# Up projection: pools laid out anew, sums of h behind h's own parts and two rows at once; down projection: low weight parts on VectorE

## The chip, the cores and the metric

The kernel runs on one core of one Trainium2 chip. The metric is the device time of one launch in microseconds. It was run three times, and the median counts.

## The reference, cut to what matters

A trunk of two layers for 1024 prompt frames and 8 x 16 sample frames (1152 columns in all, held as three chunks of 384), model width 1024, hidden width 4096. Layer 0 mixes with forgetting attention and causal pooling, layer 1 with stick-breaking attention. Behind each mixer stands the same MLP, which is what is changed:

```python
def _rmsnorm(x, g):
    xf = x.astype(jnp.float32)
    y = xf * lax.rsqrt(jnp.mean(xf * xf, axis=-1, keepdims=True) + EPS)
    return (y * g.astype(jnp.float32)).astype(x.dtype)

def _sq_relu_mlp(h, w_up, w_down):
    return jnp.square(jax.nn.relu(h @ w_up)) @ w_down
...
        h = _rmsnorm(x, norm_g[i, 1]) * (1 + sc2) + sh2
        x = x + g2 * _sq_relu_mlp(h, w_up[i], w_down[i])
```

## The kernel before

Every product is made in three passes: each fp32 operand is split into a high part (a cast on ACT) and a low part (the value less its high part, a subtraction on DVE or POOL), and PE adds high x high, high x low and low x high. The Tile framework's scheduler sets the order of each engine's queue from its own model of durations; `behind`, `at` and pins add constraints.

*Up projection* (`up_phase`, L516). The activations h lie in `xT`, feature rows on partitions, 8 rows k of 128. First the norm of each of the three chunks is made: squares on ACT (L367, L370), added up on DVE and POOL (L371) into `sa` and `sb`, joined (L372), summed over partitions by PE (L375), a square root on ACT (L381), a reciprocal on DVE (L382 to L385), and spread by PE (L392). `apply` (L533) multiplies by it on DVE (L535) and adds the shift on ACT (L536); the sample columns go through `samples` (L538) on DVE and POOL. The columns are then regrouped into four blocks of TB = 288: two halves tp, each with columns c = 1 and 2; feature rows are two halves r = 1 and 2 of four rows j.

`parts` (L546) makes a form's high part on ACT (L548) and its low part on DVE (L549), one row j at a time. The forms 11, 21, T4 and 22 are blocks of h themselves; T1, T2 and T3 come from `sums` (L567), seven-product (Strassen) sums of blocks, with subtractions on DVE (L565). The first four of 32 weight columns f are made by `plain` (L683), which needs only h's own blocks: a tile is 24 matmuls (L693), squared and clipped on ACT and DVE (L699, L700). The other 28 are taken two at a time, as 14 groups of seven products P1 to P7 (L629), each product with a weight form that DVE adds up from raw blocks (L565, L608). Raw blocks come over SP's queue (L583) into `u_raw` buffers (UR of them), and `w_parts` splits them: `u_hi` on ACT (L589), `u_lo` on POOL (L590), four buffers each. The results go to DRAM on ACT's queue (L637).

*Down projection* (`down_phase`, L765). The 32 rows f of the hidden layer are taken in rounds of (2, 2, 4, 4, 4, 4, 4, 4, 2, 2). For each f of a round SP loads the hidden row `hr` (128 x 3 x 384, three buffers) and the weight row `w_raw` (128 x 1024); `split` (L199) makes `w_hi` on ACT (L203) and `w_lo` on POOL (L204; on DVE for odd f below 4); `oh` is cast on ACT (L791), `ol` subtracted on DVE (L792), a chunk at a time; six buffers each. A pair of weight parts lies in one of three buffers of the weights' pool or three of `wx`. PE then makes 24 tiles a round (8 rows n by 3 chunks), each over all f of the round (L506), and `x_add` (L489) adds a tile to x on DVE (L492, for samples L496 and POOL's L498).

## Time and profile before

| | us |
|---|---|
| median of 3 runs (3207.66 to 3208.86) | 3208.78 |
| the profiled execution | 3204.72 |
| its span, which the trace covers | 3202.9 |
| PE busy in it | 3039.6 (95%) |
| DVE busy | 1778.7 (56%) |
| ACT busy | 1101.4 (34%) |
| POOL busy | 960.9 (30%) |

The mean granted clock of TensorE was 0.97 of full speed. Busy shares are means over stages with different limits: a stage is read from its windows (busy time of each engine and granted clock in a stretch) and from the list of waits (how long PE stood still, and what ended it). A busy PE at clock 0.50 does half the work of one at 1.00. The chain of work that ended last follows PE for the most part, so time that PE waits is time of the whole.

### The profile page before, as it was taken

What the parts mean: (1) busy time and instruction counts of PE and PEld (TensorE: products, weight loads), DVE (VectorE), ACT (ScalarE), POOL (GpSimd) and SP (SyncE); (2) the same over time, 40 slices, a digit from 0 to 9 for tenths busy, and PEclk for the clock granted to TensorE, in tenths of its full rate; (3) what the DMA queues carried; (4) which work ended last, traced back from release to release, by engine and by line L of the source; (5) the groups of instructions that cost most, each with busy time, mean ns of one, the idle gap of its engine ahead of it and who ended that gap; (6) DMA issues with size and microseconds to landing.
All of it is one profiled execution on the core that took longest, in us unless ns stands there. A gap on an engine that the chain in (4) does not pass through costs nothing. (4 is left out here: it accounts for less than half of the span.)

```text
span 3202.9 us, 54950 instructions
## 1 busy us (share of the span) xinstructions
PE 3039.6 (95%) x21422; PEld 2771.0 (87%) x21422; DVE 1778.7 (56%) x3500; ACT 1101.4 (34%) x2482; POOL 960.9 (30%) x801
## 2 busy tenths in 40 slices
PE   8999999979999999999999999999969999899898
...
GB/s 273 203 216 240 139 139 93 128 53 110 98 99 148 241 117 137 148 108 40 211 168 168 194 193 105 168 138 108 133 59 100 101 103 112 193 78 63 106 49 60
DMA packets 398792, 427.67 MB, mean 134 GB/s; under 512 B 41629, under 2 KB 349509, under 8 KB 398534
## 3 DMA queue, kind: packets, MB, share of 16 engines
...
## 5 line engine op out<-in xcount | busy, mean ns | idle before, releaser
L590 POOL TENSOR_TENSOR u_lo<-u_raw,u_hi 128x512 fp32r<-128x512 f32 x226 | 324.7, 1439 | 478.4 <-ACT u_hi L589 475.2
L204 POOL TENSOR_TENSOR w_lo<-w_raw,w_hi 128x1024 fp32r<-128x1024 f32 (+1 forms) x116 | 287.6, 2490 | 433.3 <-ACT w_hi L203 313.4
L498 POOL TENSOR_TENSOR xT<-xT,xs 128x128 f32<-128x128 f32 x224 | 117.7, 525 | 829.7 <-DVE xs L496 822.2
L203 ACT CAST w_hi<-w_raw 128x1024 fp32r<-128x1024 f32 (+1 forms) x120 | 125.7, 1051 | 645.9 <-PE ps_s L506 422.7
L492 DVE SCALAR_TENSOR_TENSOR xT<-ps_s,modT,xT 128x384 f32<-128x384 f32 (+1 forms) x372 | 210.6, 568 | 217.2 <-PE ps_s L506 215.9
L629 PE MATMUL ps_s<-FT,u_hi 128*128 128x288 f32 x1568 | 315.9, 295 | 0.0
L506 PE MATMUL ps_s<-ol,w_hi 128*128 128x384 f32 x792 | 267.7, 340 | 13.2 <-DVE ol L792 13.2
L506 PE MATMUL ps_s<-oh,w_hi 128*128 128x384 f32 x792 | 272.8, 344 | 0.7 <-DVE xT L492 0.4
L506 PE MATMUL ps_s<-oh,w_lo 128*128 128x384 f32 x792 | 270.7, 342 | 0.0
L589 ACT CAST u_hi<-u_raw 128x512 fp32r<-128x512 f32 x226 | 139.9, 621 | 354.5 <-PE ps_s L629 175.4
L629 PEld LDWEIGHTS ps_s<-FT,u_hi 128*128 128x128 f32 x1568 | 253.7, 189 | 0.0
L1173 DVE TENSOR_TENSOR_SCAN sn<-sn 128x128 f32<-128x128 f32 (+4 forms) x224 | 216.6, 995 | 45.2 <-ACT sn L1167 40.4
L629 PE MATMUL ps_s<-FT,u_lo 128*128 128x288 f32 x784 | 233.5, 298 | 4.8 <-POOL u_lo L590 4.8
L640 DVE TENSOR_TENSOR xT<-ps_s,xT 128x288 f32<-128x288 f32 x224 | 102.2, 457 | 219.1 <-PE ps_s L629 218.9
L1176 POOL TENSOR_TENSOR sg<-sg,sn 128x512 f32<-128x512 f32 (+3 forms) x112 | 136.2, 1216 | 260.6 <-DVE sn L1173 194.1
L792 DVE TENSOR_TENSOR ol<-hr,oh 128x384 fp32r<-128x384 f32 x192 | 192.0, 1053 | 19.7 <-ACT oh L791 19.6
L629 PE MATMUL ps_t<-F,u_hi 128*128 128x288 f32 x896 | 180.3, 294 | 2.6 <-ACT xT L656 2.6
L1241 ACT COPY pt<-ps_t 128x512 f32<-128x512 f32 (+3 forms) x256 | 126.2, 500 | 128.7 <-PE ps_t L1235 127.1
L492 DVE SCALAR_TENSOR_TENSOR xT<-ps_a,modT,xT 128x384 f32<-128x384 f32 (+1 forms) x180 | 102.2, 568 | 122.5 <-PE ps_a L506 121.8
L506 PE MATMUL ps_s<-w_hi,h 128*128 128x256 f32 (+1 forms) x800 | 159.2, 291 | 6.1 <-ACT h L466 3.4
L506 PEld LDWEIGHTS ps_s<-ol,w_hi 128*128 128x128 f32 x792 | 150.4, 190 | 15.7 <-DVE ol L792 15.7
L506 PEld LDWEIGHTS ps_s<-oh,w_hi 128*128 128x128 f32 x792 | 150.4, 190 | 14.8 <-issue 5.9
...
## 6 DMA issues: line engine op xcount, KB each, us to landing
...
```

Of the source, the lines that this page charges most:

```text
L203: after(nc.scalar.copy(hi[:, :n], raw[:, :n]), "act")
L204: after((eng or nc.gpsimd).tensor_tensor(lo[:, :n], raw[:, :n], hi[:, :n].bitcast(F32), op=ALU.subtract), "pool")
L492: nc.vector.scalar_tensor_tensor(xT[c][:, n, :npc], ps[:, :npc], g[:, n, 0:1], xT[c][:, n, :npc], op0=ALU.mult, op1=ALU.add)
L498: nc.gpsimd.tensor_tensor(xT[c][:, n, 256:], xT[c][:, n, 256:], t, op=ALU.add)
L506: mm = nc.tensor.matmul(ps, lhsT=a, rhs=b, start=(i == 0), stop=(i == n - 1))
L589: nc.scalar.copy(hi, src)
L590: nc.gpsimd.tensor_tensor(lo, src, hi.bitcast(F32), op=ALU.subtract)
L629: mm = nc.tensor.matmul(ps, lhsT=a[:, k, :], rhs=b[:, k, :], start=(start and i == 0), stop=(i == 11), skip_group_check=not start)
L792: nc.vector.tensor_tensor(ol[:, c], raw[:, c], oh[:, c].bitcast(F32), op=ALU.subtract)
L1173: nc.vector.tensor_tensor_scan(rev, rev, rev, initial=1.0, op0=ALU.mult, op1=ALU.bypass)
L1176: eng.tensor_tensor(sg[:, 0:m - 1], sg[:, 0:m - 1], sn[:, 1:m], op=ALU.mult)
L1241: nc.scalar.copy(pt.rearrange("p k n -> p (k n)")[:, 0:n], T[:, 0:n])
```

## The change

In the up projection: `apply` takes a whole chunk instead of pieces of 96 to 288 columns; `parts` and the sums take two rows j at once, so there are half as many, twice as wide; the first three subtractions of `sums` are put `behind` the latest low part of h's own blocks (`done["lo"]`); the norm's squares have two buffers; `u_raw` has five; and the pools are opened in another order and on other sides of the memory, with `u_out` in one of its own. In the down projection every `w_lo` of a hidden row is made on DVE, `wx` is used by f // 2, and `oh` and `ol` are made for all three chunks in one operation (in the first round in two). In the forget-attention one pool moves to the left side. The diff, without its blank lines:

```diff
@@ -62,7 +62,7 @@
 PIN_O = (5, 15)
 PIN_M = (4, 11)
 TB = 288
-UR = 6
+UR = 5
 UW = 4
 UG = 2
 UO = 3
@@ -521,18 +521,31 @@
         w = w_up[l]
         forms = ("11", "21", "T2", "T1", "T3", "22", "T4")
         with ExitStack() as es:
-            ur = es.enter_context(tc.tile_pool(name=f"ur{l}", bufs=1, side="right", reuse_waits="tile"))
-            uf = [es.enter_context(tc.tile_pool(name=f"uf{l}{tp}", bufs=1, reuse_waits="tile",
-                                                **({"side": "right"} if tp == 0 else {}))) for tp in range(2)]
-            uw = es.enter_context(tc.tile_pool(name=f"uw{l}", bufs=UW, side="right", reuse_waits="tile"))
-            F = {f: [[uf[tp].tile([P, 4, TB], F32R, name=f"F{f}{i}", tag=f"F{f}{i}") for i in range(2)] for tp in range(2)]
-                 for f in forms}
-            np_ = Npool(ur, {"sa": 1, "sb": 1, "nw": 1, "rc": 2})
-            def apply(c, sd, k, c0, c1):
-                x = xT[c][:, k, c0:c1]
-                nc.vector.scalar_tensor_tensor(x, x, A[:, k, 0:1], sd[:, c0:c1], op0=ALU.mult, op1=ALU.mult)
+            def pool(name, side="left", bufs=1):
+                return es.enter_context(tc.tile_pool(name=f"{name}{l}", bufs=bufs, side=side, reuse_waits="tile"))
+            def form_tiles(pools):
+                return {f: [pl.tile([P, 4, TB], F32R, name=f"F{f}{i}", tag=f"F{f}{i}") for i in range(2)] for f, pl in pools.items()}
+            ufa = pool("ufa")
+            F1 = form_tiles({f: ufa for f in forms[:4]})
+            uo = pool("uo")
+            uo.tile([P, TB], F32, name="u_out", tag="out", bufs=UO)
+            uw = pool("uw", bufs=UW)
+            ufb = pool("ufb")
+            F1.update(form_tiles({f: ufb for f in forms[4:]}))
+            ur = pool("ur", "right")
+            uf = pool("uf", "right")
+            F0 = form_tiles({f: uf for f in forms})
+            F = {f: (F0[f], F1[f]) for f in forms}
+            np_ = Npool(ur, {"sa": 1, "sb": 1, "nw": 2, "rc": 2})
+            def apply(c, sd, k):
+                x = xT[c][:, k, :CW if c < 2 else 256]
+                nc.vector.scalar_tensor_tensor(x, x, A[:, k, 0:1], sd[:, :CW if c < 2 else 256], op0=ALU.mult, op1=ALU.mult)
                 nc.scalar.activation(x, x, AF.Identity, bias=B[:, k, 0:1])
             def samples(sd, k0, k1):
@@ -544,37 +557,37 @@
                 nc.gpsimd.tensor_tensor(w4, w4, B[:, k0:k1, 1:9].unsqueeze(3).broadcast_to([P, n, NB, NT]), op=ALU.add)
             def parts(form, tp, j, src):
-                hi, lo = (t[:, j, :] for t in F[form][tp])
+                hi, lo = (t[:, j:j + 2, :] for t in F[form][tp])
                 nc.scalar.copy(hi, src)
-                nc.vector.tensor_tensor(lo, src, hi.bitcast(F32), op=ALU.subtract)
+                return nc.vector.tensor_tensor(lo, src, hi.bitcast(F32), op=ALU.subtract)
             def blk(tp, j, r, c):
                 t0 = (2 * tp + c - 1) * TB
-                return X[:, j + 4 * (r - 1), t0:t0 + TB]
-            def first_forms(tp, j):
-                parts("11", tp, j, blk(tp, j, 1, 1))
-                parts("21", tp, j, blk(tp, j, 2, 1))
-            def second_forms(tp, j):
-                parts("T4", tp, j, blk(tp, j, 1, 2))
-                parts("22", tp, j, blk(tp, j, 2, 2))
+                return X[:, j + 4 * (r - 1):j + 4 * (r - 1) + 2, t0:t0 + TB]
+            FIRST = {(1, 1): "11", (2, 1): "21", (1, 2): "T4", (2, 2): "22"}
+            def plain_parts(tp, c, k):
+                r, j = k // 4 + 1, k % 4
+                done["lo"] = parts(FIRST[r, c], tp, j, blk(tp, j, r, c))
+            done = {}
             def sub(o, a, b):
-                nc.vector.tensor_tensor(o, a, b, op=ALU.subtract)
+                return nc.vector.tensor_tensor(o, a, b, op=ALU.subtract)
             def sums(tp, j):
                 b11, b12, b21, b22 = (blk(tp, j, r, c) for r in (1, 2) for c in (1, 2))
-                sub(b11, b12, b11)
-                sub(b12, b22, b12)
-                sub(b22, b22, b11)
+                for o, x, y in ((b11, b12, b11), (b12, b22, b12), (b22, b22, b11)):
+                    behind(sub(o, x, y), done["lo"])
                 parts("T2", tp, j, b22)
                 parts("T1", tp, j, b11)
                 parts("T3", tp, j, b12)
                 sub(b21, b21, b22)
-            KO = (0, 4, 1, 5, 2, 6, 3, 7)
+            KO = (0, 4, 2, 6)
             def raw_block(g, r, c):
@@ -695,7 +708,7 @@
                                     behind(mm, last["mm"])
                                 n += 1
                     last["mm"] = mm
-                    t = ur.tile([P, TB], F32, name="u_out", tag="out", bufs=UO)
+                    t = uo.tile([P, TB], F32, name="u_out", tag="out", bufs=UO)
                     nc.scalar.activation(t, ps, AF.Relu)
                     nc.vector.scalar_tensor_tensor(t, ps, 0.0, t, op0=ALU.max, op1=ALU.mult)
                     out({"g": f // 2, "tp": tp}, f % 2 + 1, c, t)
@@ -706,46 +719,39 @@
             ws = plain_weights((0, 1))
             with at(0):
                 sd = rstd_of(0, np_, 0)
-                for i, k in enumerate(KO):
-                    apply(0, sd, k, 0, TB)
-                    if i % 2:
-                        first_forms(0, i // 2)
+                for k in KO:
+                    apply(0, sd, k)
+                    apply(0, sd, k + 1)
+                    plain_parts(0, 1, k)
             plain((0, 1), ws, 0, 1)
             with at(1):
-                sd1 = rstd_of(1, np_, 1)
-                h1 = 2 * TB - CW
-                for i, k in enumerate(KO):
-                    apply(0, sd, k, TB, CW)
-                    apply(1, sd1, k, 0, h1)
-                    if i % 2:
-                        second_forms(0, i // 2)
+                sd = rstd_of(1, np_, 1)
+                for k in KO:
+                    apply(1, sd, k)
+                    apply(1, sd, k + 1)
+                    plain_parts(0, 2, k)
             pins.clear()
             plain((0, 1), ws, 0, 2)
-            sd2 = rstd_of(2, np_, 2)
-            for i, k in enumerate(KO):
-                apply(1, sd1, k, h1, CW)
-                apply(2, sd2, k, 0, 3 * TB - 2 * CW)
-                if i % 2:
-                    first_forms(1, i // 2)
+            sd = rstd_of(2, np_, 2)
+            for k in KO:
+                apply(2, sd, k)
+                apply(2, sd, k + 1)
+                plain_parts(1, 1, k)
+                samples(sd, k, k + 2)
             plain((0, 1), ws, 1, 1)
-            for i, k in enumerate(KO):
-                apply(2, sd2, k, 3 * TB - 2 * CW, 256)
-                if i % 2 == 0:
-                    samples(sd2, i // 2 * 2, i // 2 * 2 + 2)
-            for j in range(4):
-                second_forms(1, j)
+            for k in KO:
+                plain_parts(1, 2, k)
             plain((0, 1), ws, 1, 2)
-            fill = [(tp, j) for tp in range(2) for j in range(4)]
+            fill = [(tp, j) for tp in range(2) for j in (0, 2)]
             for f in range(2, 2 * UG, 2):
                 ws = plain_weights((f, f + 1))
                 for tp in range(2):
                     for c in (1, 2):
-                        for _ in range(2):
-                            if fill:
-                                sums(*fill.pop(0))
+                        if fill:
+                            sums(*fill.pop(0))
                         plain((f, f + 1), ws, tp, c)
             for tp in range(2):
-                for j in range(4):
+                for j in (0, 2):
                     parts("T4", tp, j, blk(tp, j, 2, 1))
             NG = FF // P // 2
@@ -785,11 +791,11 @@
                 for f in range(f0, f0 + r):
                     raw = hr.tile([P, NCH, CW], F32, name="hr", tag="hr", bufs=3)
                     nc.sync.dma_start(raw.rearrange("p c n -> p (c n)"), hid_sc[f // 2][f % 2])
-                    ws.append(load_rows(w_down[l], f * P, wx if f % 2 else None, nc.vector if f % 2 and f0 < 4 else nc.gpsimd))
+                    ws.append(load_rows(w_down[l], f * P, wx if f // 2 % 2 else None, nc.vector))
                     oh, ol = (hid.tile([P, NCH, CW], F32R, name=n, tag=n, bufs=HB) for n in ("oh", "ol"))
-                    for c in ((2, 1, 0) if f0 == 0 else range(NCH)):
-                        nc.scalar.copy(oh[:, c], raw[:, c])
-                        nc.vector.tensor_tensor(ol[:, c], raw[:, c], oh[:, c].bitcast(F32), op=ALU.subtract)
+                    for cs in ((slice(2, 3), slice(0, 2)) if f0 == 0 else (slice(0, NCH),)):
+                        nc.scalar.copy(oh[:, cs], raw[:, cs])
+                        nc.vector.tensor_tensor(ol[:, cs], raw[:, cs], oh[:, cs].bitcast(F32), op=ALU.subtract)
                     hs.append((oh, ol))
                 if last:
                     order = [(c, n) for c in range(NCH) for n in range(KD)]
@@ -1066,7 +1072,7 @@
                 fo = ph2.enter_context(tc.tile_pool(name="fo", bufs=1, side="right", reuse_waits="tile"))
             hd2 = ph2.enter_context(tc.tile_pool(name=f"hl{l}", bufs=1, side="right", reuse_waits="tile"))
             if fox:
-                hd = ph2.enter_context(tc.tile_pool(name=f"hd{l}", bufs=2, side="right", reuse_waits="tile"))
+                hd = ph2.enter_context(tc.tile_pool(name=f"hd{l}", bufs=2, reuse_waits="tile"))
                 Fst = fo.tile([P, NP_], F32R, name="Fst")
                 selp = fo.tile([P, 8], F32R, name="selp")
                 nc.vector.tensor_copy(selp, cst[:, C_SELP:C_SELP + 8])
```

What it moves on the engines, at three places. The first is DVE's queue at the start of layer 0's up projection, around the norm of the third chunk (`sa<-sa,nw` are its additions). `xT<-xT` are the subtractions of `sums`, `F_` and `FT_` low parts of the forms. Before:

```order
L549 TENSOR_TENSOR F_7069<-xT,F_7068 128x288
L565 TENSOR_TENSOR xT<-xT 128x288 x3
L549 TENSOR_TENSOR FT_7061<-xT,FT_7060 128x288
L371 TENSOR_TENSOR sa<-sa,nw 128x384
L565 TENSOR_TENSOR xT<-xT 128x288
L549 TENSOR_TENSOR FT_7061<-xT,FT_7060 128x288 x2
L565 TENSOR_TENSOR xT<-xT 128x288
L700 SCALAR_TENSOR_TENSOR u_out<-ps_t,u_out 128x288
```

After, the additions are in front and the sums stand behind the parts of the second half; this is where that half's parts end and the sums begin (`128x2x288` is an operation on two rows; before, `128x288` was one on one row):

```order
L562 TENSOR_TENSOR F_7040<-xT,F_7039 128x576
L562 TENSOR_TENSOR FT_7062<-xT,FT_7061 128x576
L562 TENSOR_TENSOR F_7042<-xT,F_7041 128x576
L562 TENSOR_TENSOR F_7060<-xT,F_7059 128x576
L579 TENSOR_TENSOR xT<-xT 128x2x288 x6
L562 TENSOR_TENSOR FT_7076<-xT,FT_7075 128x576
L579 TENSOR_TENSOR xT<-xT 128x2x288
L562 TENSOR_TENSOR FT_7076<-xT,FT_7075 128x576
L579 TENSOR_TENSOR xT<-xT 128x2x288
```

So no sum is left between h's own parts.

The second is ACT's queue at the start of layer 1's up projection. `u_hi` are the high parts of the first weights. Before, 24 applies (L536) and eight casts of forms stand ahead of the first of them; this is where they end:

```order
L548 CAST F_25217<-xT 128x288
L548 CAST F_25213<-xT 128x288
L548 CAST F_25217<-xT 128x288
L548 CAST FT_25237<-xT 128x288
L589 CAST u_hi<-u_raw 128x512
L548 CAST F_25233<-xT 128x288
L589 CAST u_hi<-u_raw 128x512 x3
L548 CAST FT_25237<-xT 128x288
L548 CAST F_25233<-xT 128x288
```

After, the same four stand among the squares of the norm (`nw`, `sa`, `sb`):

```order
L367 ACTIVATE sa<-xT 128x384
L164 COPY AT<-ps_t 16x128
L367 ACTIVATE sb<-xT 128x384
L370 ACTIVATE nw<-xT 128x384 x2
L602 CAST u_hi<-u_raw 128x512
L370 ACTIVATE nw<-xT 128x384
L602 CAST u_hi<-u_raw 128x512
L370 ACTIVATE nw<-xT 128x384
L602 CAST u_hi<-u_raw 128x512
L370 ACTIVATE nw<-xT 128x384
L602 CAST u_hi<-u_raw 128x512
```

So the four casts moved from behind the applies to ahead of them.

The third is DVE's queue at a boundary between two rounds of four in layer 1's down projection. Before:

```order
L492 SCALAR_TENSOR_TENSOR xT<-ps_t,modT,xT 128x384
L792 TENSOR_TENSOR ol<-hr,oh 128x384
L492 SCALAR_TENSOR_TENSOR xT<-ps_s,modT,xT 128x256
L496 TENSOR_TENSOR xs<-ps_s,modT 128x128
L792 TENSOR_TENSOR ol<-hr,oh 128x384 x11
L492 SCALAR_TENSOR_TENSOR xT<-ps_a,modT,xT 128x384
```

After:

```order
L492 SCALAR_TENSOR_TENSOR xT<-ps_t,modT,xT 128x384
L204 TENSOR_TENSOR w_lo<-w_raw,w_hi 128x1024
L492 SCALAR_TENSOR_TENSOR xT<-ps_s,modT,xT 128x256
L496 TENSOR_TENSOR xs<-ps_s,modT 128x128
L798 TENSOR_TENSOR ol<-hr,oh 128x1152
L204 TENSOR_TENSOR w_lo<-w_raw,w_hi 128x1024
L798 TENSOR_TENSOR ol<-hr,oh 128x1152
L204 TENSOR_TENSOR w_lo<-w_raw,w_hi 128x1024
L798 TENSOR_TENSOR ol<-hr,oh 128x1152 x2
L204 TENSOR_TENSOR w_lo<-w_raw,w_hi 128x1024
L492 SCALAR_TENSOR_TENSOR xT<-ps_a,modT,xT 128x384
```

Where twelve `ol` pieces stood, there are four whole ones and four `w_lo`, which were on POOL before.

## Rows read from the trace of the kernel before

**Rows 1.** The page: busy us of each engine (share of the span) and instructions.

```profile
PE 3039.6 (95%) x21422; PEld 2771.0 (87%) x21422; DVE 1778.7 (56%) x3500; ACT 1101.4 (34%) x2482; POOL 960.9 (30%) x801
```

**Rows 2.** Waits of PE, whole span: us in total, times, longest.

```profile
PE ps_t L693 <- DVE F L549: 16.2, 8, 3.8
...
PE ps_s L506 <- DVE ol L792: 13.2, 8, 1.9
PE ps_t L693 <- POOL u_lo L590: 12.3, 1, 12.3
PE ps_t L506 <- DVE ol L792: 11.2, 7, 1.8
PE ps_t L693 <- ACT u_hi L589: 10.9, 1, 10.9
PE ps_a L506 <- ACT oh L791: 9.9, 2, 5.2
...
PE ps_a L506 <- DVE ol L792: 5.6, 9, 2.0
...
PE ps_s L629 <- POOL u_lo L590: 4.8, 2, 2.6
```

**Rows 3.** Windows, up projection start, layer 0: length, busy per engine, clock, DMA share, GB/s.

```profile
640.00:650.00 10.00, 3.67 (x10) 2.41 (x10) 10.00 (x33) 10.00 (x31) 1.52 (x2) 0.71 0.06 21
...
660.00:670.00 10.00, 5.09 (x39) 4.80 (x37) 9.69 (x28) 2.98 (x8) 1.65 (x1) 0.91 0.14 46
670.00:680.00 10.00, 4.04 (x13) 3.04 (x13) 8.39 (x25) 8.04 (x26) 5.30 (x8) 0.50 0.05 16
```

**Rows 4.** Timelines, up projection start, layer 1: start, length, work, [idle before].

```profile
2332.45 0.85 PE L693 MATMUL ps_t<-F,u_hi 128*128 128x288 f32 x2 [10.94 <-ACT u_hi L589]
2345.64 0.61 PE L693 MATMUL ps_t<-F,u_lo 128*128 128x288 f32 x1 [12.33 <-POOL u_lo L590]
...
2331.49 3.03 DVE L549 TENSOR_TENSOR F<-xT,F 128x288 fp32r<-128x288 f32 x8
...
2332.48 16.80 POOL L590 TENSOR_TENSOR u_lo<-u_raw,u_hi 128x512 fp32r<-128x512 f32 x4 [3.99 <-ACT u_hi L589]
```

**Rows 5.** Timeline of DVE, into the down projection of layer 0: three pieces.

```profile
1034.75 2.28 DVE L204 TENSOR_TENSOR w_lo<-w_raw,w_hi 128x1024 fp32r<-128x1024 f32 x1
...
1041.04 1.23 DVE L204 TENSOR_TENSOR w_lo<-w_raw,w_hi 128x1024 fp32r<-128x1024 f32 x1 [0.62 <-ACT w_hi L203]
1042.76 2.90 DVE L792 TENSOR_TENSOR ol<-hr,oh 128x384 fp32r<-128x384 f32 x6 [0.49 <-ACT oh L791]
```

**Rows 6.** Timelines and windows, a round boundary of the down projection, layer 1.

```profile
2956.17 1.05 ACT L203 CAST w_hi<-w_raw 128x1024 fp32r<-128x1024 f32 x1 [46.84 <-PE ps_s L506]
...
2967.29 0.44 PE L506 MATMUL ps_s<-ol,w_hi 128*128 128x384 f32 x1 [1.84 <-DVE ol L792]
...
2960.64 11.57 DVE L792 TENSOR_TENSOR ol<-hr,oh 128x384 fp32r<-128x384 f32 x10
...
2961.46 7.99 POOL L204 TENSOR_TENSOR w_lo<-w_raw,w_hi 128x1024 fp32r<-128x1024 f32 x3
...
2965.00:2970.00 5.00, 1.32 (x7) 0.69 (x5) 5.00 (x3) 1.34 (x3) 4.45 (x2) 0.87 0.05 22
2970.00:2975.00 5.00, 5.00 (x16) 5.00 (x17) 4.84 (x11) 0.00 (x0) 0.46 (x1) 0.50 0.81 264
```

**Rows 7.** Waits of PE, down projection of layer 1 with its lead-in (2785 to 3110).

```profile
PE ps_s L506 <- DVE ol L792: 9.2, 5, 1.8
PE ps_t L506 <- DVE ol L792: 9.2, 5, 1.8
```

**Rows 8.** Timelines of POOL, DVE, ACT, one Strassen group of layer 0.

```profile
818.88 1.29 POOL L590 TENSOR_TENSOR u_lo<-u_raw,u_hi 128x512 fp32r<-128x512 f32 x1 [2.32 <-ACT u_hi L589]
...
820.65 0.69 DVE L565 TENSOR_TENSOR u_raw<-u_raw 128x512 f32<-128x512 f32 x1 [0.94 <-DMA u_raw<-in_w_up_dram]
...
823.93 0.62 ACT L589 CAST u_hi<-u_raw 128x512 fp32r<-128x512 f32 x1 [2.55 <-PE ps_a L629]
```

## The prediction

> **What bounds the kernel now.** I first read the page's list of engines: PE is busy for 3039.6 of 3202.9 us and no other engine for more than 56% [rows 1], so time can only come from places where PE waits or runs at the lower clock. The list of PE's waits then names the places [rows 2]. The three on DVE's `ol` sum to 30.0 us and belong to the down projections. At L693, the first plain products of the up projections, PE waits 16.2 us for the low parts of h, 10.9 for a weight's high part and 12.3 for its low part. Two waits on `oh` (9.9) and two on POOL's `u_lo` (4.8) lie where the up projection hands over to the down projection. These are the places that the diff touches.
>
> Then I read each stretch. In layer 0, PE is busy for 3.67, 5.09 and 4.04 us in three of the 10 us windows at the start of the up projection, with granted clocks of 0.71, 0.91 and 0.50 [rows 3]: 17.2 us idle, and about 1.1 + 0.5 + 2.0 us of busy time lost to the lower level (1.2 GHz, against 2.4). DVE is busy for nearly all of two of these windows, so DVE's queue is the bound there. In layer 1, PE issues two matmuls at 2332.45 and the third at 2345.64 [rows 4]. POOL's four `u_lo` lasted 16.80 us there, while one alone takes 1.29 [rows 8]: the first needed about 16.80 - 3 x 1.29 = 12.9 us. In that time DVE ran 34 operations with two SBUF inputs without a gap (the first eight are shown). So POOL starves beside such a row.
>
> In the down projection the wait sits at the boundaries between rounds. ACT is idle 46.84 us until PE frees the weights, then everything for the next round comes at once [rows 6]. POOL's three `w_lo` last 7.99 us (2.66 each), and ten `ol` of DVE last 11.57, against 2.90 for six where POOL is quiet [rows 5]. PE loses 3.7 us of the 5 us window and runs the next 5 us at clock 0.50, another 2.5. In layer 1 this comes five times, with the same longest wait of 1.8 each [rows 7].
>
> The Trainium skill ("SBUF — State Buffer", Who interferes with whom) says that a DVE instruction with two SBUF inputs contends with a GpSimd instruction that reads SBUF, and that whoever comes first keeps the shared port for a whole instruction. The trace agrees in [rows 4, 6], with 12.9 us for 1.29 and 1.16 for 0.48. By that rule a two-row subtraction keeps the port for longer at a time; the first rival below prices that from rows.
>
> **The change part by part.**
>
> Estimates of sizes first. DVE's 288-column subtraction follows at 3.03 / 8 = 0.38 us [rows 4], the 384-column one at 2.90 / 6 = 0.48 [rows 5]: 0.10 per 96 columns. So 576 columns cost about 0.69, and 1152 about 1.28, against 3 x 0.48 = 1.45 in pieces. `w_lo` is 1.23 alone and 2.28 at worst [rows 5].
>
> 1. *Up projection, start, layer 0.* Sixteen applies of 384 columns now stand ahead of the first low part, where there were eight of 288: 16 x 0.48 - 8 x 0.38 = 4.6 us later. In return the low parts of the first half come two rows at a time with no smaller applies between them, so that PE no longer stalls inside those tiles; I take the end of this half at 1 us earlier. The large piece is the third chunk. Before, its norm's additions stood among the sums of the first half (order, first place), and from 660 to 680 PE lost 4.9 + 6.0 us idle and 2.5 to the clock: 13.4. After, DVE has only the chain itself: eight applies at about 0.4, four products for the samples at 0.35 and one low part, 5.3 us, and I leave 1 us of stalls behind it. That gives 13.4 - 6.3 = 7; with the 1 us, and 1 of the lower clock just behind 680, 9 us less. Bounds: 5 (the clock stays low) and 13.4.
>
> 2. *The same, layer 1.* ACT's casts of the weights move from behind 24 applies and 8 casts to among the squares of the norm (order, second place), and POOL's `u_lo` with them. Of the 10.94 us wait little is pure gain: DVE's first low part began only at 2331.49 [rows 4]. But the third matmul need no longer wait until 2345.64. First low part after: the same sixteen applies first, so no later than before, at about 2330. Gain 2345.6 - 2330 = 15.6; I take 16 with the lower clock. Bounds: 10 (the third chunk's chain is more exposed, since less of it is hidden behind the long wait) and 23.3, both waits whole.
>
> 3. *Sums behind h's parts.* 28 sums and parts of 0.69 = 19 us on DVE, moved to after the second half's parts. They are first used by the Strassen products, behind eight more plain tiles, so they are covered. POOL's `u_lo` for the next two rows of weights fall into this stretch. The nearest row is the starved one, 12.9 for 1.29 [rows 4], and an excess of 11.6 with one plain tile as its cover (24 matmuls of about 0.14 = 3.4) leaves 8.2 per layer at worst; below nothing it can't be, for a `u_lo` that isn't blocked was hidden already. DVE's evacuations, which wait for PE, stand among the sums and let POOL in. I take 2 per layer, +4, bounds 0 to 16.
>
> 4. *Five buffers for raw weights instead of six.* The difference s2 of a group now takes the buffer of the previous group's a22, which P4's `u_lo` reads last. That read is over at 820.17, before's s2 ran at 820.65 and its reader at 823.93 [rows 8]: 823.93 - 820.17 - 0.69 = 3.1 us of slack. Nothing.
>
> 5. *Down projection: `w_lo` on DVE, `ol` whole.* Per row of weights DVE takes 1.23 + 1.28 = 2.5 us instead of three pieces of up to 1.16 (3.5), and POOL's 2.66 go. At a boundary DVE's queue is `w_lo`, a PSUM evacuation or two, `ol`, `w_lo`, `ol` (order, third place). From the release: ACT's `w_hi` 1.05, `w_lo` 1.23, evacuations 0.9, `ol` 1.28 = 4.5 us. In the changed order 46 matmuls stand between the last reader of the oldest `oh` and the first reader of the third new `ol`; at 5.00 / 16 / 2 = 0.16 us each at full clock [rows 6] that is 7.2 us. The second pair ends at 4.5 + 2.5 = 7.0, against 57 matmuls, 8.9 us. So spare 1.9 to 2.7 us, and no wait. Layer 1: five times 3.7 + 2.5 is 31; I take -30 (bounds 0 and -33). Layer 0: 30.0 - 18.4 [rows 7] leaves 11.6 us of waits for layer 0 and small ones; POOL still has weights of the next layer to split there; I take -8 (0 to -12).
>
> 6. *Hand-over.* The two waits on `u_lo`, 4.8, came from POOL's `w_lo` in front of it and go. But three `w_lo` stand ahead of the first `ol`, up to 3.7 us. I take -4 for both layers, bounds -14.7 (both `oh` waits too) and +3.
>
> 7. *Forget-attention's pool on the other side.* SP now issues part of K and Q behind two loads for the output projection. PE's order puts the first scores a few matmuls later as well; no row prices this. I take 0, between -2 and +5.
>
> Sum: -9 - 16 + 4 + 0 - 30 - 8 - 4 + 0 = **-63**. Against the profiled execution, 3204.7 - 63 = 3141.7; it stands 4.1 below the median of the runs, so the median becomes 3208.8 - 63 = 3146.
>
> **The rivals.**
>
> *The two-row sums starve POOL.* Step 3 at its upper bound, in both layers: +12, and some lower clock behind it: 3161. For it speaks [rows 4]. Against it: the evacuations among the sums.
>
> *Whole-row operations come too late.* The Trainium skill ("Perfetto Trace Analysis", Optimizing Scalar/DVE Operations) says that where an engine is not saturated but makes others wait, smaller instructions may get work done sooner. DVE is at 56% and PE waits for it, so this speaks against the whole-row `ol`. In rows: a first piece of `ol` took 0.48, a whole row takes 1.28, 0.8 later, and as much again for ACT's cast. If the spare 1.9 is used up by something else, each of 18 boundaries (nine per layer) loses 1.6: +29, 3175.
>
> *The change doesn't do what it says.* If `u_lo` of layer 1 is starved in its new place too (DVE adds the norm's squares there, with two SBUF inputs each), steps 1 and 2 shrink to some 5 us in all: 3166, or 3185 with the boundaries half cured.
>
> *Slower: DVE's one queue holds up every boundary.* If `w_lo` takes 2.28 and `ol` 3 x 1.16 = 3.5 even so, the chain is 1.05 + 2.28 + 0.9 + 3.5 = 7.7, and the second pair ends at 13.5 against 8.9: 4.6 us late, 18 times 83 us, where the down projections now lose 30 + 13 (clock). That is +40 there, -25 elsewhere: 3224. It is slower from 3.8 us late per boundary, (43 + 25) / 18. Against it: POOL, which makes those durations, has no more splitting to do in layer 1.
>
> **How the numbers follow.** Forecast 0.62 (own range 3125 to 3165), starved POOL 0.12 (3161), late whole rows 0.12 (3175), change not doing it 0.05 (3166 to 3205), slower 0.05 (3224), and 0.04 for more gain than forecast, all good bounds together (3115). The range 3116 to 3184 leaves out the slower case and the tails. A measurement of this kernel can tell about 0.2% from no change, 6.4 us. Faster: 0.92; same 0.03, the tail of the fourth case; slower 0.05.
>
> **What would show it.** PE's waits after: no L693 wait over 4 us on `u_lo` or `u_hi`; no wait of 1.8 on `ol` in layer 1, and no window at clock 0.50 behind its boundaries; `ol` at about 1.3 and `w_lo` at about 1.2 us on DVE. In the start of layer 0, the third chunk's wait is under 7 us. A row of `u_lo` over 5 us beside the sums would be the first rival; waits on `ol` that remain at 1 to 2 us the second; `w_lo` of over 2 us on DVE the last. I would be most wrong if PE's order in the changed boundaries no longer hides the evacuations that wait behind DVE's 10 us of parts.

## The result and the profile after

The changed kernel takes 3152.3 us (3149.9 to 3155.6), the kernel before 3208.2 beside it: ratio 0.9826, 95% interval 0.9809 to 0.9843. The forecast of 3146 was 6 us too low, inside its range and on the right side. The profiled execution has a span of 3148.1 us, 54.8 less than before.

The page's list of engines and the first of PE's waits over the whole span, after (us in total, times, longest), answer to [rows 1, 2]:

```profile
PE 3016.8 (96%) x21422; PEld 2755.3 (88%) x21422; DVE 1767.2 (56%) x3292; ACT 1071.8 (34%) x2246; POOL 812.5 (26%) x741
...
PE ps_t L706 <- DVE F L562: 19.1, 6, 6.6
PE ps_a L506 <- ACT oh L797: 13.1, 2, 6.8
PE ps_a L375 <- DVE sa L372: 10.2, 3, 5.3
PE ps_t L706 <- ACT F L561: 9.3, 4, 2.9
```

The waits on `ol`, 30.0 us before, are gone; no row of PE's waits names it. What was not cured stands in front: h's parts (L706, was 16.2) and `oh` at the hand-over (was 9.9).

To place the 54.8 us I cut both traces at the starts of the same instructions: first apply of each up projection, first and last Strassen matmul, first matmul of the down projection, and its last `ol` on DVE (what PE still does behind layer 0's last `ol`, some 50 us, counts with the mixer). Lengths in us; e1 and e12 are experiments below.

| stretch | before | after | change | forecast | e1 | e12 |
|---|---|---|---|---|---|---|
| to the first apply, layer 0 (forget-attention) | 637.8 | 647.8 | +10.0 | 0 | 635.3 | 632.3 |
| up projection's start, layer 0 | 82.5 | 80.5 | -2.0 | -9 and +2 | 84.1 | 82.0 |
| Strassen products, layer 0 | 317.4 | 316.2 | -1.2 | 0 | 316.2 | 316.2 |
| hand-over, layer 0 | 5.1 | 6.6 | +1.5 | -2 | 6.6 | 4.7 |
| down projection, layer 0 | 407.5 | 392.7 | -14.8 | -8 | 392.7 | 392.1 |
| mixer of layer 1 | 869.5 | 874.9 | +5.3 | 0 | 871.9 | 874.4 |
| up projection's start, layer 1 | 93.4 | 79.0 | -14.4 | -16 and +2 | 78.6 | 73.4 |
| Strassen products, layer 1 | 318.2 | 316.1 | -2.1 | 0 | 316.2 | 316.1 |
| hand-over, layer 1 | 5.7 | 7.1 | +1.4 | -2 | 6.9 | 7.3 |
| down projection, layer 1, and the end | 465.8 | 427.3 | -38.5 | -30 | 427.7 | 426.1 |

The down projection gave more than forecast, forget-attention took 10 us, and the first layer's start gave little. A boundary of the second layer, after: windows (length; busy us of each engine; granted clock, DMA share, GB/s) and pieces of DVE's timeline (start, length, work), the answer to [rows 6]:

```profile
2870.00:2875.00 5.00, 5.00 (x30) 5.00 (x29) 2.02 (x3) 1.87 (x2) 0.00 (x0) 1.00 0.00 0
2875.00:2880.00 5.00, 5.00 (x31) 5.00 (x30) 5.00 (x7) 4.24 (x5) 1.50 (x1) 1.00 0.58 156
2880.00:2885.00 5.00, 5.00 (x30) 5.00 (x29) 3.52 (x3) 2.17 (x2) 0.00 (x0) 1.00 0.97 338
```

```profile
2875.95 1.35 DVE L798 TENSOR_TENSOR ol<-hr,oh 128x1152 fp32r<-128x1152 f32 x1
2877.21 1.48 DVE L204 TENSOR_TENSOR w_lo<-w_raw,w_hi 128x1024 fp32r<-128x1024 f32 x1
...
2883.84 1.36 DVE L798 TENSOR_TENSOR ol<-hr,oh 128x1152 fp32r<-128x1152 f32 x1 [1.48 <-ACT oh L797]
```

PE is busy throughout at full clock, where it lost 3.7 us of a window and then ran at 0.50 before.

### The profile page after: what moved, and what is told of

It is laid out like the page before. It is cut to its first block, busy times and chain, and to the rows that moved or that the text cites. A ratio compares the mean times of both kernels' runs of the same rounds, so it can differ in the third digit from the quotient of the medians.

```text
span 3148.1 us, 54306 instructions
## 1 busy us (share of the span) xinstructions
PE 3016.8 (96%) x21422; PEld 2755.3 (88%) x21422; DVE 1767.2 (56%) x3292; ACT 1071.8 (34%) x2246; POOL 812.5 (26%) x741
## 4 chain that ended last, share of the span: by engine, by line
PE 59%; DVE 5%; issue 1%; DMA 1%; POOL 1%; ACT 1%; ACTq 0%; SPq 0%; DVEq 0%; POOLq 0%
PE ps_s L506 20%; PE ps_a L506 9%; PE ps_t L506 9%; PE ps_s L642 6%; PE ps_t L642 3%; PE ps_a L1261 2%; PE ps_t L1241 2%; PE ps_a L642 1%; DVE sn L1179 1%; PE ps_s L1225 1%; PE ps_m L251 1%; PE ps_s L1320 1%; PE ps_s L1226 1%; PE ps_m L1308 1%; PE ps_t L706 1%
## 5 line engine op out<-in xcount | busy, mean ns | idle before, releaser
L603 POOL TENSOR_TENSOR u_lo<-u_raw,u_hi 128x512 fp32r<-128x512 f32 x226 | 309.6, 1373 | 413.1 <-ACT u_hi L602 408.2
L498 POOL TENSOR_TENSOR xT<-xT,xs 128x128 f32<-128x128 f32 x224 | 131.1, 585 | 1000.6 <-DVE xs L496 994.8
L204 POOL TENSOR_TENSOR w_lo<-w_raw,w_hi 128x1024 fp32r<-128x1024 f32 (+1 forms) x56 | 134.3, 2406 | 357.0 <-ACT w_hi L203 189.5
L506 PEld LDWEIGHTS ps_s<-oh,w_hi 128*128 128x128 f32 x792 | 150.2, 190 | 14.4 <-DVE xs L496 5.9
L1261 PE MATMUL ps_a<-pt,V 128*64 128x128 f32 x1728 | 155.0, 283 | 0.0
L899 DVE TENSOR_TENSOR kt<-ps_t,kt 128x512 fp32r<-128x512 f32 x24 | 16.6, 691 | 238.9 <-ACT kt L898 238.9
```

What stands on the lines that cost most here:

```text
L204: after((eng or nc.gpsimd).tensor_tensor(lo[:, :n], raw[:, :n], hi[:, :n].bitcast(F32), op=ALU.subtract), "pool")
L498: nc.gpsimd.tensor_tensor(xT[c][:, n, 256:], xT[c][:, n, 256:], t, op=ALU.add)
L506: mm = nc.tensor.matmul(ps, lhsT=a, rhs=b, start=(i == 0), stop=(i == n - 1))
L603: nc.gpsimd.tensor_tensor(lo, src, hi.bitcast(F32), op=ALU.subtract)
L1261: nc.tensor.matmul(A[rs, os_], lhsT=Vd[kb // 4][:, kb % 4, rs], rhs=PTs[h2][kb], start=(kb == 0), stop=(kb == i))
```

## The experiments

Every edit makes the scheduler order the whole program anew, and stretches that an edit doesn't touch move by some 5 us either way (the Strassen products of layer 0 by 5.2 between e5 and e7, for one). Each stretch is from one profiled execution. So I read an effect in its own stretch first and in the total second, and trust none below about 5 us in one stretch, unless several kernels show it alike or the waits of PE name it. Ratios are to the kernel before, with 95% intervals.

### Which edit of the down projection counts

**e3_down_only**: the kernel before with the down projection's edit alone.

```
-  ws.append(load_rows(..., wx if f % 2 else None, nc.vector if f % 2 and f0 < 4 else nc.gpsimd))
+  ws.append(load_rows(..., wx if f // 2 % 2 else None, nc.vector))
-  for c in ((2, 1, 0) if f0 == 0 else range(NCH)):
+  for cs in ((slice(2, 3), slice(0, 2)) if f0 == 0 else (slice(0, NCH),)):
       (oh and ol over cs instead of c)
```

> The kernel before with the edits of the down projection only (low weight parts on DVE, the weights' pools used by f // 2, oh and ol made whole). Theory: the down projections carry nearly all of the gain: 14 us less in layer 0 and 38 in layer 1, and 1 to 3 us more in the hand-overs, about 3157 us. Rival (the up projection's start and the down projection share it evenly): 3175 to 3185 us.

Measured 3157.2 us, 0.984 (0.9823 to 0.9856), as expected. Down projections and the end: -15.7 and -39.7 us.

**e4_wlo_only**: only the first two lines of that diff; `ol` stays in pieces.

> The kernel before with the low weight parts of the down projection on DVE (and the weights' pools by f // 2), but oh and ol in three pieces of 384 columns each as before. Theory: what made PE wait was that POOL's splitting and DVE's ol held each other up; without it the pieces take 0.48 to 0.55 us, DVE needs 2.7 instead of 2.5 us per row of weights, and nearly the whole gain is here: 3157 to 3162 us, no waits of 1.8 us on ol in layer 1. Rival: the whole-row operations carry it, since three pieces and a weight part in DVE's queue are too many at a boundary: 3175 us or more, with waits on ol that remain.

Measured 3158.7 us, 0.9842 (0.9828 to 0.9857): all of the gain with half of the edit, as my theory had it.

**e8_ol_only**: only the other half, whole rows of `oh` and `ol`; POOL goes on making `w_lo`.

> The kernel before with oh and ol made whole, while POOL still makes the low weight parts. Theory: the whole row alone doesn't help, because POOL's splitting still holds up DVE's subtractions at the boundaries: waits of 1.5 us and more on ol remain in layer 1, 3195 to 3212 us. Rival: half as many takings of the port are enough: 3175 us or less.

Measured 3155.6 us, 0.9836 (0.982 to 0.9852). Here my theory fell: POOL still splits every weight, each `ol` is still held up (2.2 us on average instead of 1.38), and yet no wait on `ol` is left. Either half is enough. So "POOL must go" is not the cause, and three readings remained: the length of POOL's turns, the number of DVE's pieces, or the whole `oh`. The next two runs test the first and the last; a whole `ol` without the whole `oh` was not run.

**e9_wlo_quarters**: the kernel before, POOL making each `w_lo` of the down projection as four pieces.

```
-  after((eng or nc.gpsimd).tensor_tensor(lo[:, :n], raw[:, :n], hi[:, :n]..., op=ALU.subtract), "pool")
+  for a in range(0, n, n // cut):                      (cut = 4 on POOL in the down projection)
+      b = a + n // cut
+      after((eng or nc.gpsimd).tensor_tensor(lo[:, a:b], raw[:, a:b], hi[:, a:b]..., op=ALU.subtract), "pool")
```

> The kernel before, with one change: where the down projection makes a w_lo on POOL, it makes it in four pieces of 128x256 instead of one of 128x1024; oh and ol stay in pieces of one chunk. Undone in neither of the two edits that were enough alone (w_lo to VectorE, or ol as whole rows). Theory 'length of a turn': each of the ten small ol at a boundary (11.57 us for ten of about 0.6 us) lost its turn to a whole w_lo of some 2.7 us; against pieces of about 0.7 us (a quarter of 2.66, or half of u_lo's 1.44 for 512 columns) it loses at most 0.7 a piece, ten pieces take 6 to 9 us in place of 11.6, and most of PE's 53 us of waits for ol goes: 3157 to 3178 us, and next to no L506<-DVE ol waits left. Rival 'sum of the work': the two engines' time at a boundary is what counts, and it is the same: waits stay near 30 us or more in the second layer, 3195 to 3215 us; POOL's pieces may even cost more in sum (226 u_lo of 512 columns take 1.44 us, a w_lo of 1024 2.49, so small pieces are dearer per column).

Measured 3157.7 us, 0.9846 (0.9829 to 0.9863): all of the gain again, with POOL doing the same columns and DVE the same pieces.

**e10_oh_whole**: the kernel before, `oh` as whole rows on ACT, `ol` still in pieces.

```
+  cs = (2, 1, 0) if f0 == 0 else range(NCH)
-  for c in ((2, 1, 0) if f0 == 0 else range(NCH)):
+  for c in ((slice(2, 3), slice(0, 2)) if f0 == 0 else (slice(0, NCH),)):
       nc.scalar.copy(oh[:, c], raw[:, c])
+  for c in cs:
       nc.vector.tensor_tensor(ol[:, c], ...)
```

> The kernel before, with ScalarE's oh made as one whole row (the first as chunk 2 and then chunks 0 and 1), VectorE's ol still in pieces of one chunk, w_lo on POOL as before. Half of the edit that brought 53 us alone. Theory 'pieces on VectorE': the count of small ol that each meet a w_lo sets the wait, and it is the same; 3195 to 3212 us, with some 30 us of PE's waits for ol in the second layer as before. Rival 'order and start of oh': the whole oh on ScalarE is due with its row's first piece, so that all ol of a row can start together and earlier, and this moves them away from the w_lo: 3175 us or less, and no waits for ol.

Measured 3198.7 us, 0.9973 (0.9962 to 0.9983), and the waits on `ol` fell only from 30.0 to 24.3. By itself the whole `oh` is worth about 9 us, not the 53.

Groups of instructions by line (engine, work, count | busy us, mean ns | idle before), of before, e8 and e9 in this order:

```profile
L204 POOL TENSOR_TENSOR w_lo<-w_raw,w_hi 128x1024 fp32r<-128x1024 f32 x114 | 282.4, 2488 | 425.7 <-ACT w_hi L203 305.8 <-PE ps_a L506 115.0 <-DVE sm L1009 4.8
L792 DVE TENSOR_TENSOR ol<-hr,oh 128x384 fp32r<-128x384 f32 x192 | 192.0, 1053 | 19.7 <-ACT oh L791 19.6
```

```profile
L204 POOL TENSOR_TENSOR w_lo<-w_raw,w_hi 128x1024 fp32r<-128x1024 f32 x114 | 302.8, 2667 | 419.4 <-ACT w_hi L203 264.3 <-PE ps_a L506 138.8 <-PE ps_t L506 16.2
L792 DVE TENSOR_TENSOR ol<-hr,oh 128x1152 fp32r<-128x1152 f32 x60 | 131.4, 2216 | 16.3 <-ACT oh L791 16.3
```

```profile
L206 POOL TENSOR_TENSOR w_lo<-w_raw,w_hi 128x256 fp32r<-128x256 f32 x240 | 211.6, 914 | 82.4 <-ACT w_hi L203 82.4
L794 DVE TENSOR_TENSOR ol<-hr,oh 128x384 fp32r<-128x384 f32 x192 | 155.0, 860 | 21.5 <-ACT oh L793 21.4
```

One boundary of the second layer, DVE's timeline, of before, e10, e9 and e8:

```profile
2957.67 2.45 DVE L792 TENSOR_TENSOR ol<-hr,oh 128x384 fp32r<-128x384 f32 x1 [1.27 <-ACT oh L791]
...
2960.64 12.04 DVE L792 TENSOR_TENSOR ol<-hr,oh 128x384 fp32r<-128x384 f32 x11
```

```profile
2900.27 13.63 DVE L794 TENSOR_TENSOR ol<-hr,oh 128x384 fp32r<-128x384 f32 x12
```

```profile
2881.96 0.79 DVE L794 TENSOR_TENSOR ol<-hr,oh 128x384 fp32r<-128x384 f32 x1 [1.36 <-ACT oh L793]
...
2883.26 10.42 DVE L794 TENSOR_TENSOR ol<-hr,oh 128x384 fp32r<-128x384 f32 x11
```

```profile
2880.53 7.45 DVE L792 TENSOR_TENSOR ol<-hr,oh 128x1152 fp32r<-128x1152 f32 x3
...
2889.43 2.03 DVE L792 TENSOR_TENSOR ol<-hr,oh 128x1152 fp32r<-128x1152 f32 x1 [1.45 <-ACT oh L791]
```

From the first `ol` to the end of the last this is 15.0, 13.6, 11.7 and 10.9 us, and 9.3 in the changed kernel. The first two wait for `ol`, the others don't, and it is the same at all five boundaries of this layer: there the cover that PE has ends somewhere between 11.7 and 13.6 us. It is not one number for every boundary: in layer 0 a row of 13.5 us in e9 brought no wait, and one of 10.7 before brought one of 0.5. For the second layer, then, the loss was a margin overrun by a few us; each edit that takes 3 us off DVE's row gets under it, and the second one then has nothing left to give (e3 with both, 3157.2, is no faster than e4 or e8).

### Forget-attention's pool

**e1_hd_right**: the changed kernel, the pool `hd` back where it was.

```
-  hd = ph2.enter_context(tc.tile_pool(name=f"hd{l}", bufs=2, reuse_waits="tile"))
+  hd = ph2.enter_context(tc.tile_pool(name=f"hd{l}", bufs=2, side="right", reuse_waits="tile"))
```

> The changed kernel with the forget-attention's small pool back on the right side, all else as changed. Theory: the pool's move alone made the forget-attention start some 9 us later (its first score products stand at 311.9 instead of 306.3 us, and the first apply of layer 0's up projection 10 us later), because K, V and Q are now loaded behind two weight loads that wait for POOL. Then this runs at about 3143 us, and the first score products are back near 306 us. Rival: the later start has to do with the order that the scheduler finds for the whole program, not with this pool; then it stays at 3150 to 3154 us.

Measured 3135.0 us, 0.9769 (0.9754 to 0.9783): faster than both kernels, by 17 us against the changed one, where my theory had 9. The first score product stands at 308.1 us, the first apply 12.5 us earlier.

**e2_hd_left_only**: the kernel before with that one line changed the other way, and nothing else.

> The kernel before with this one pool moved to the left side and nothing else. Theory: about 3217 us, 9 slower than before, all of it lost between 280 and 430 us. Rival (the pool alone costs nothing): 3207 to 3210 us.

Measured 3224.2 us, 1.0048 (1.0033 to 1.0063): 15 us slower, not 9. The first score product stands at 317.1 us and the first apply comes 14.9 us later; the start behind it takes 8.3 longer, against my theory, with waits of 14.4 and 7.9 us for the first `u_hi` and `u_lo`. In the totals both runs give the pool's move one price: 15 to 17 us. Timelines of SP's queue, of before and after:

```profile
280.60 6.41 SPq L1209 DMA_DIRECT2D Q<-q  x4
...
292.88 2.77 SPq L236 DMA_DIRECT2D w_raw<-in_w_out_ab_dram  x2
```

```profile
294.27 2.68 SPq L236 DMA_DIRECT2D w_raw<-in_w_out_ab_dram  x2
301.89 0.80 SPq L1195 DMA_DIRECT2D K<-k  x2
302.75 0.43 SPq L1200 DMA_DIRECT2D V<-v  x1
303.22 7.42 SPq L1215 DMA_DIRECT2D Q<-q  x4
```

Windows behind it, of before and after:

```profile
300.00:310.00 10.00, 8.98 (x57) 7.50 (x55) 6.18 (x10) 2.47 (x5) 2.67 (x2) 1.00 0.81 281
310.00:320.00 10.00, 7.61 (x95) 6.74 (x95) 7.29 (x18) 2.73 (x5) 0.00 (x0) 0.83 0.84 288
```

```profile
300.00:310.00 10.00, 5.82 (x41) 4.82 (x39) 6.54 (x10) 2.46 (x5) 2.66 (x2) 0.93 0.96 332
310.00:320.00 10.00, 5.57 (x80) 3.70 (x80) 4.45 (x11) 3.90 (x7) 0.00 (x0) 0.67 1.00 336
320.00:330.00 10.00, 9.31 (x42) 8.94 (x43) 3.93 (x12) 1.61 (x5) 0.00 (x0) 0.72 0.96 296
```

The loads of Q, 280.60 before, stand behind two loads for the output projection and go out at 303.22. PE has little to do from 300 to 320, and its clock falls for the window behind too. In e1 the loads of Q start at 282.21 again and the window from 310 reads 7.63 at 0.88.

The place in the queue is not the whole cause. The two weight loads are out by 296.95, and the first load of K into the moved pool goes out at 301.89. What SP waits for in between, after (240 to 345):

```profile
SPq L1195 <- PE ps_t L506: 4.9, 1, 4.9
```

What ends this wait is a product of the input projections that reads `h`, and it ends at 301.87; in e2 such a product ends at 307.11 and the load of K goes out at 307.14. `h` lies in a pool on the left side, so the moved pool very likely gets memory that `h` held until then; the addresses themselves are not in the trace.

### The start of the up projection

e1 leaves a wait of 12.9 us for `u_hi` in layer 0. I took it for a wait until PE had last read the output projection's operands, where the tiles of `u_hi` lie. The trace says otherwise: PE's last product of that projection ends at 635.6 and PE idles from 636.3 to 649.1, while ACT works from 635.90 without a gap on sixteen applies, seven casts of h's forms and one square, and only then, at 648.46, comes to the four `u_hi`. So what ends the wait is `u_hi`'s place in ACT's queue.

**e5_uw_moved**: e1 with the up projection's left pools in another order, so that `uw` lies elsewhere.

```
    uo.tile([P, TB], F32, name="u_out", ...)      (unchanged)
+   ufb = pool("ufb")                              (now ahead of uo)
    uw = pool("uw", bufs=UW)
-   ufb = pool("ufb")
```

> As e1_hd_right, and in the up projection the pools of the weights' parts and of the results are opened behind the forms' second pool instead of ahead of it, so that the weights' parts no longer lie where the output projection's operand lay. In e1 PE waited 12.9 us for the first u_hi in layer 0, which had to wait for the output projection's last reads. Theory: with that memory conflict gone the wait goes and layer 0's up start (84.1 us from the first apply to P1 in e1) comes to about 76 to 79 us: 3127 to 3131 us in all. Rival: the 12.9 us only hid the third chunk's norm and the parts of h, and the start stays at 82 to 84 us: 3134 to 3137 us.

Measured 3145.4 us, 0.9804 (0.979 to 0.9819): a miss. The wait is gone (with the pools elsewhere the scheduler puts `u_hi` at 615.5) and layer 0's start is 4.2 us shorter, but the stretch ahead of it is 3.6 longer, Strassen 2.8 in layer 0, the hand-overs 1.3 and 3.1, layer 1's start 4.3. The 12.9 us had covered other lateness: PE now waits 9.4 us for the low and 4.1 for the high parts of h there, against 3.0 and 2.2 in e1. Why the rest moved is open.

**e6_no_behind**: e5 without `behind(...)` around the three subtractions in `sums`. **e7_one_row**: e5 with parts and sums one row at a time.

> As e5_uw_moved, without the constraint that puts the sums behind h's own low parts. Theory: the constraint pays, as the prediction took it: without it the sums of the first half stand ahead of the third chunk's norm again and the start of each layer's up projection gets 3 to 5 us longer than in e5. Rival: in the changed kernel DVE idles for some 9 us between 666 and 676 us while PE works off the first half, and pays later, when 19 us of sums make POOL's u_lo last 10.8 us for four and PE waits 3.4; without the constraint the sums fill that gap, no u_lo wait of 3 us remains, and it is 3 to 5 us shorter per layer than e5.

> As e5_uw_moved, with parts and sums of h made one row at a time (twice as many operations, half as wide). Theory: two rows at once save DVE only 0.09 us a pair (2 x 0.37 against 0.67, 64 pairs in both layers, 6 us of DVE time), and the first low part comes 0.3 us later; the time is within 4 us of e5 either way. Rival 1 (the wide operations keep POOL from its port and cost PE its u_lo wait): 3 to 6 us faster than e5. Rival 2 (DVE's time at the start is all on the path): 6 us slower than e5 or more.

Measured 3149.2 us (0.9817, 0.9802 to 0.9832) and 3142.6 us (0.9797, 0.9783 to 0.9812). Starts of the two layers: 79.9 and 82.9 us in e5, 78.8 and 84.9 without `behind`, 74.6 and 80.4 in single rows, where the Strassen products of layer 0 take back 5.2. In total neither part is worth more than about 4 us, of either sign.

Cut finer, the two say more. The sums stand beside the last 192 of a start's 384 plain matmuls. In the kernel before these take 25.4 us in both layers and PE never waits in them; in the changed kernel, e1, e5 and e11, with two rows at once behind h's parts, they take 29.1 to 32.5. Without `behind` they take 25.3 and 25.4, in single rows 25.3 and 27.2. So most of that price, some 4 us a layer, takes both parts together. Without `behind` it comes back elsewhere: the 96 matmuls ahead of these, the ones with the third chunk, take 28.0 and 25.6 us against 24.6 and 24.7 in e5, and in layer 1 the wait for `u_hi` grows from 7.0 to 12.8, which I can't trace to `behind`.

**e11_hr_ulo_dve**: e1 with eight `u_lo` per layer, beside the sums, on VectorE.

```
-  return {f: [w_parts(raw_block(f // 2, f % 2 + 1, c)) for c in (1, 2)] for f in fs}
+  return {f: [w_parts(raw_block(f // 2, f % 2 + 1, c), nc.vector if f > 1 else nc.gpsimd) for c in (1, 2)] for f in fs}
```

> The changed kernel with Fox's hd pool on the right as in the kernel before (that run: 3135 us), and the u_lo of the third and fourth row of the up projection's first weights (eight per layer) on VectorE in place of POOL. Theory: PE's one wait for u_lo in the first layer (3.4 us in the changed kernel, POOL's u_lo x4 taking 10.81 us beside the sums) goes, as VectorE and POOL no longer work against each other there; VectorE has 8 x 0.8 to 1.2 us more per layer, some of it in front of sums or first parts. 3129 to 3136 us. Rival: VectorE is the engine that PE waits for in this stretch (19.1 us in six waits), and the eight take their whole time from it: 3138 to 3150 us.

Measured 3139.5 us, 0.9787 (0.9772 to 0.9802), against e1's 0.9769: no gain. PE's wait for `u_lo` only changed its engine, from 6.4 us on POOL to 6.3 on DVE and 1.3 on POOL.

**e12_norm_first**: e1, with the third chunk's norm written ahead of the second half's plain products.

```
   pins.clear()
-  plain((0, 1), ws, 0, 2)
   sd = rstd_of(2, np_, 2)
+  plain((0, 1), ws, 0, 2)
```

> The changed kernel with Fox's hd pool on the right (3135 us), and the third chunk's norm statistics and scale written ahead of the second half of the first plain products, so that PE's three L375 and three L392 stand some 46 matmuls earlier and VectorE need not stand still for PE between the parts of the second chunk and the applies of the third (it stood idle from 665.8 to 676.1 in the changed kernel's first layer, waiting for u_out's tiles). Theory: this is where step 1 lost its gain; VectorE's third-chunk work starts up to 9 us earlier, the waits of PE for F in both layers (9.3 and 19.1 us in all) fall by 5 to 12 us: 3123 to 3131 us, and the first layer's start shorter than 84 us and the second's shorter than 78.6. Rival: the statistics delay PE's first plain products, or the first parts of the second chunk are what PE needs next and the applies of the third chunk now stand before them: 3135 to 3146 us.

Measured 3128.5 us, 0.9754 (0.9739 to 0.9769): the fastest of all, 80 us under the kernel before. In totals it lies 5 to 6.5 us under e1, and half of its interval lies in e1's; in its own stretches the starts fall from 84.1 and 78.6 to 82.0 and 73.4. DVE's timeline where it changes, layer 0, e1 and then e12:

```profile
668.66 0.87 DVE L548 SCALAR_TENSOR_TENSOR xT<-xT,Ad,ps_a 128x256 f32<-128x256 f32 x2 [1.03 <-PE ps_a L392]
```

```profile
663.15 0.87 DVE L548 SCALAR_TENSOR_TENSOR xT<-xT,Ad,ps_a 128x256 f32<-128x256 f32 x2 [1.49 <-PE ps_a L392]
```

Counted from the first apply, the third chunk's applies begin at 33.4 us in e1 and 30.9 in e12: of the 9 us that I allowed, 2.5 came. Nor is this where most of the gain lies. Of the 7.3 us of both starts, the 96 matmuls with the third chunk gave 3.7 and the 192 beside the sums 5.6 (there PE's waits for `u_lo` fell from 2.1 and 3.0 us to 1.1 and 0.2), and the first half lost 1.9.

## Why the prediction was right, and where it wasn't

**Steps 1 and 3, layer 0: -9 and +2 forecast, -2.0 measured.** I cut the start at the 96th and the 192nd of its 384 plain matmuls, into the first half, the third chunk and the sums: 26.4 + 30.7 + 25.4 us before, 27.8 + 22.4 + 30.3 after. The third chunk gave 8.3, as forecast (7, and 1 of the clock). Two terms failed: the first half, "I take the end of this half at 1 us earlier", ends 1.4 later, and the sums, "I take 2 per layer", cost 4.9. DVE's timeline after:

```profile
647.82 4.28 DVE L548 SCALAR_TENSOR_TENSOR xT<-xT,Ad,ps_a 128x384 f32<-128x384 f32 x8
...
657.28 2.09 DVE L562 TENSOR_TENSOR F<-xT,F 128x576 fp32r<-128x576 f32 x3
...
676.11 0.46 DVE L713 SCALAR_TENSOR_TENSOR u_out<-ps_s,u_out 128x288 f32<-128x288 f32 x1 [2.71 <-ACT u_out L712]
676.48 0.86 DVE L548 SCALAR_TENSOR_TENSOR xT<-xT,Ad,ps_a 128x256 f32<-128x256 f32 x2
```

An apply of 384 columns takes 0.53 us, not 0.48, and an evacuation of the output projection and a norm's addition stand between the sixteen, so the first low part starts 9.5 us after the first apply. Before, it started 6.0 us after it: sixteen applies stood ahead of it there too, eight of them narrower, and not eight as I had read. PE waits 2.9 and 6.6 us in this half, where it had waited 8.0 in five pieces. DVE then stands in its queue for the evacuations of these tiles, with the third chunk's applies behind them. The third chunk itself was sized well: from 670 to 690 PE is idle 3.3 + 2.2 us and loses 2.6 to the clock, 8.2 in place of 13.4:

```profile
670.00:680.00 10.00, 6.69 (x50) 6.29 (x48) 4.57 (x13) 3.80 (x9) 2.09 (x4) 1.00 0.14 46
680.00:690.00 10.00, 7.76 (x37) 6.95 (x38) 8.78 (x14) 6.43 (x12) 5.97 (x5) 0.66 0.00 0
```

The sums' price was over twice my 2: POOL's four `u_lo` take 10.81 us, the first of them 5.53, PE waits 3.4 and then loses 1.5 to the clock. Windows beside the sums, of before and after, POOL's timeline after, and PE's waits from 640 to 735 after:

```profile
695.00:700.00 5.00, 5.00 (x40) 5.00 (x39) 5.00 (x11) 1.68 (x4) 1.83 (x2) 1.00 0.61 168
700.00:705.00 5.00, 5.00 (x40) 5.00 (x39) 2.07 (x6) 0.90 (x3) 0.00 (x0) 1.00 0.42 137
```

```profile
695.00:700.00 5.00, 3.24 (x25) 3.01 (x23) 5.00 (x9) 4.49 (x10) 3.93 (x1) 1.00 0.09 31
700.00:705.00 5.00, 3.34 (x15) 3.35 (x16) 5.00 (x5) 1.19 (x2) 5.00 (x3) 0.66 0.34 101
```

```profile
696.07 10.81 POOL L603 TENSOR_TENSOR u_lo<-u_raw,u_hi 128x512 fp32r<-128x512 f32 x4 [9.95 <-ACT u_hi L602]
```

```profile
PE ps_t L706 <- DVE F L562: 9.7, 3, 6.6
PE ps_t L706 <- ACT F L561: 5.2, 2, 2.9
PE ps_t L706 <- POOL u_lo L603: 3.4, 1, 3.4
```

e7, in single rows, is without this price here (25.3 us); e12 brings the third chunk forward and gains less there than beside the sums.

**Step 2, layer 1: -16 and +2 forecast, -14.4 measured.** The step is right, the sum by luck. In the same three parts, 40.9 + 27.0 + 25.4 us became 24.6 + 24.3 + 30.1: the first half gave 16.3, as forecast; the third chunk gave 2.7, which I had not counted; and the sums cost 4.7 instead of 2. Beside the sums it is DVE that is late here: two low parts took 3.62 us while POOL made `u_lo`, against 0.75 for one elsewhere, and PE waited 3.0 for an evacuation that stands behind the sums on ACT and DVE. The waits of 10.9 and 12.3 for `u_hi` and `u_lo` are gone; 9.4 for F on DVE (was 4.6), 4.1 on ACT and 3.0 for an evacuation have come. PE's waits from 2310 to 2400, after:

```profile
PE ps_t L706 <- DVE F L562: 9.4, 3, 6.5
PE ps_t L706 <- ACT F L561: 4.1, 2, 2.2
PE ps_t L706 <- DVE u_out L713: 3.0, 1, 3.0
```

**Step 4: nothing forecast.** The Strassen products are 1.2 and 2.1 us shorter, less than I trust. Right.

**Step 5: -38 forecast, -53.3 measured (-14.8 and -38.5).** The place was right and the size low. Adding up the 5 us windows of before, PE loses 21.4 us idle and 13.8 us to the lower clock from 2740 to 3110, at five boundaries, and 9.2 and 5.1 from 1045 to 1450, at three; after, 0.7 us to the clock in the second layer and 0.5 in the first (from 1055 on, behind the hand-over). That is 35 and 14 us, the bulk of the 53, where I had 30 and 8. For layer 0 I had counted the waits that are listed under `ol` and not the clock behind them; its stretch is 14.8 us shorter, though the mixer behind it is 5.3 longer for a reason that I didn't find. The mechanism as I told it, POOL and DVE holding each other up, was half of it: e9 and e8 keep POOL at work and lose nothing. What the runs show is that the row of `ol` ends too late when small pieces meet long turns of POOL, and that mending either side is enough. `w_lo` takes 1.28 and `ol` 1.38 us on DVE, as estimated.

**Step 6: -4 forecast, +2.9 measured.** The waits on `u_lo` went, but `oh` comes later. In layer 0 SP issues the first load of `hr` at 1044.60, behind two weights and seven loads of `xT`, and before at 1036.34; the last Strassen product starts at 1044.4 and 1037.7. So the load goes out 0.2 us behind that product instead of 1.4 ahead of it, 1.6 later, as much as the hand-over grew. I had priced DVE's queue and not SP's. Both hand-overs together are less than what I trust in one stretch. PE's waits there, of before (1034 to 1050) and after (1040 to 1056):

```profile
PE ps_a L506 <- ACT oh L791: 4.6, 1, 4.6
PE ps_s L629 <- POOL u_lo L590: 2.1, 1, 2.1
```

```profile
PE ps_a L506 <- ACT oh L797: 6.3, 1, 6.3
```

**Step 7: 0 forecast, bounds -2 and +5; it costs 10 us in its stretch and 15 to 17 in all** (e1, e2). With step 5 this is the largest error. The order showed K and Q behind two loads of `w_raw`, and I wrote that no row priced it. Part of the price stood in the trace: those loads go out at 292.88 before, 12 us behind the first Q, and whatever is moved behind them starts no earlier. The other part I never asked for: what last reads the memory that the moved pool gets. K waited for a product that reads `h` until 301.87, and in the trace before PE reads `h` until 303.6.

**The rivals.** Starved POOL came in part: by my own sign (a row of `u_lo` over 5 us beside the sums, here 10.81), and with 9.6 us in both layers where I had 4 and the rival 16; in layer 1 it is DVE that was held up. Whole rows too late: no wait on `ol` is left. The Trainium skill ("Perfetto Trace Analysis", Optimizing Scalar/DVE Operations), named with that rival, says that smaller instructions may get work done sooner where an engine is not saturated but makes others wait. Here the trace says the opposite for DVE, for e8's whole rows end 4 us sooner than before's pieces, while on POOL e9's small pieces did help. One queue on DVE: `w_lo` stays at 1.28, not 2.28. All good bounds together come to 98 us, so 3110 and not the 3115 that I wrote; nothing hangs on it. The errors of +10 (step 7), +7 (6) and +5 (1 and 3 in layer 0) against -15 (5) nearly cancel, with +5 in the mixer and -3 in the Strassen products. That the total is only 6 us off (8 by the profiled executions) is partly luck.
